# Two parts of the activations in one product of 512 columns: w_out, w_xq, w_xo and w_down of a decoder block

## The chip, the cores and the metric

The kernel runs on one core of a Trainium2 chip. The metric is the device time of one execution, in microseconds (us); of several runs the median is given. Engines go by the profile's names: PE is TensorE's products, PEld its loads of stationary operands, DVE is VectorE, ACT ScalarE, POOL GpSimd, SP SyncE, which issues most transfers.

## What is computed

One block over 256 rows of width 1024, in float32: a mixer (pool groups beside causal attention), cross-attention over a memory of 256 rows, and a gated feed-forward net with a convolution of three taps. Each part adds to the residual x:

```python
x = x + concatenate([pool, attn], axis=-1) @ w_out        # 1024 x 1024
h = rms_norm(x, norm_xattn_g)
x = x + cross_attention(h, m, w_xq, w_xkv, ..., w_xo)      # q = h @ w_xq; ... o @ w_xo, both 1024 x 1024
h = rms_norm(x, norm_ffn_g)
x = x + conv_ffn(h, w_up, conv_w, conv_b, w_down)          # up: 1024 x 5632; (silu(gate) * val) @ w_down: 2816 x 1024
```

## The kernel before

PE multiplies in float32r, which keeps fewer bits than float32. So each operand is split into a high part h (the value cast to float32r) and a low part l (what is left), and a product is three: h by h, h by l and l by h. ACT casts the high part and DVE subtracts for the low part, for activations (`part_h`, `part_l`, L237 to L247) and for weights alike (`split_h`, L185; `split_l`, L196). Weights come as `wpack`, chunks of two units; a unit is 128 x 1024, eight blocks of 128 x 128. `need(u)` (L198) issues transfers and splits ahead of unit u, by `look` units.

The stages of this text keep activations transposed: a feature block of 128 partitions by 256 rows (S). `b_tile` (L691) makes one output block f: for each of 8 input blocks k (22 in w_down) it calls `three`, whose products are L256 (weights' h by activations' h), L257 (weights' h by activations' l) and L258 (weights' l by activations' h). The weights are the stationary operand, the activations stream, 256 columns at a time, and all 24 (66) products go to one half of a bank of PSUM. Eight banks take turns. Pairs of activations live in two sets of four buffers, one for h and one for l (`pair`).

What empties a bank:

- w_out and w_xo, `resid_stage` (L702): DVE adds the bank to the residual (L709); ACT and DVE split the result times a gain into the next stage's operand (`evac_split`, ACT L241, DVE L247); ACT squares it (L712, L715); POOL sums the squares over the blocks (L716).
- w_xq (the loop before `value_job`): ACT and DVE split the bank straight into xq (L241, L247); ACT squares it (L801), POOL adds pairs of squares (L805).
- w_down (the last loop): DVE adds the bank and the residual into o (L936), and SP stores o (L937).

The order is by program: each engine does what it is given in that order. Work aside from the products (scores, softmax, splits of other tiles, the row sums over all blocks, L272) lies in generators, which are moved one step on by `tick()`, called after every second input block, and which wait so many ticks as the tables `WAIT_...` say. The row sums of w_out's squares are issued right behind the first output block of w_xq; those of w_xo's squares six ticks into w_up. The key job, which runs beside w_out, has DVE scale keys (L659), PE transpose them (L667) and ACT and DVE split them. An order of the stages: w_in, keys, w_out, w_xq, the value chunk (L357, L358, L361: products of 512 columns, where weights stream), w_xo, w_up, w_down.

Of the kernel before, what the change touches and what calls it, by code (L numbers as in the profile page):

```python
# [16 lines left out]
P = 128  # L17
# [8 lines left out]
XH = 4  # L26
# [48 lines left out]
def block_kernel(ctx: ExitStack, tc: tile.TileContext, wpack: bass.AP, scal: bass.AP, memT: bass.AP,  # L75
# [22 lines left out]
        return temps.tile([P, S], F32, name=name, tag="t1", bufs=8)  # L98

    def pair(name, cols=KT * S):  # L100
        h = pairs.tile([P, cols], F32R, name=name + "_h", tag="ph", bufs=4)
        l = pairs.tile([P, cols], F32R, name=name + "_l", tag="pl", bufs=4)
        return h, l

    def sm(name, n, dtype=F32):
        return small.tile([P, n], dtype, name=name)
# [147 lines left out]
    def three(o, stat, mov, start, stop):  # L254
# [2 lines left out]
        pe.matmul(o, stat[0], mov[1], start=False, stop=False)  # L257
        pe.matmul(o, stat[1], mov[0], start=False, stop=stop)  # L258

    def col(t, c):  # L260
        return t[:, c:c + 1]

    def tiles(p, k=KT):
        return [t.rearrange("p (k s) -> p k s", k=k) for t in p]

    rows = {}

# [66 lines left out]
    load_chunk(2, (0, 1024, 2048))  # L334
    nc.sync.dma_start(tab, table)
    nc.sync.dma_start(sc[:, C_GMEM:], scal[:, C_GMEM:])
    xgv = tiles(pair("xg"))

    def first_splits():
        for k in range(KT):  # L340
# [9 lines left out]
    def a_chunk(u0, actv, bk):  # L350

        for k in range(KT):
            w = need(u0 + k // 2)
            wv = [t[:, (k % 2) * 512:(k % 2) * 512 + 512] for t in w]
            a = [[t[:, k, tt * P:(tt + 1) * P] for t in actv] for tt in range(TT)]
            for tt in range(TT):
                pe.matmul(bk[tt], a[tt][0], wv[0], start=k == 0, stop=False)  # L357
                pe.matmul(bk[tt], a[tt][1], wv[0], start=False, stop=False)  # L358
            tick()
            for tt in range(TT):  # L360
                pe.matmul(bk[tt], a[tt][0], wv[1], start=False, stop=k == KT - 1)  # L361
            tick()
# [74 lines left out]
            pool.tensor_scalar(sneg, s, -(HD ** -0.5), None, op0=ALU.mult)  # L437
        yield from wait(WAIT_QK[5])

    qk = pairs.tile([P, KT * S], F32, name="qkT", tag="ph", bufs=4)  # L440
    j_of = {"q": 0, "k": 1}

    def stat_job():
# [33 lines left out]
            yield from wait(WAIT_MEM[0])  # L477
            part_l(mgv[1][:, k], r, mgv[0][:, k], col(sc, C_GMEM + k))

    mgv = tiles(pair("mg"))  # L480
    job_v = go(v_job())
    job_m = go(mem_job())
    stat_m = go(row_stat("m", mem_tile))
# [97 lines left out]
    bu = [bank(), bank()]  # L581
    look[0] = LOOKS[3]
    a_chunk(12, xgv, bu)
    cat = tiles(pair("cat"))


    def pool_job():
# [89 lines left out]
    look[0] = LOOKS[4]  # L677
    a_chunk(18, mgv, bk0)
    finish(job_k)
    kxv = tiles(pair("kx"))  # L680
    job_key0 = go(key_job(0, bk0))
    bk1 = [bank(), bank()]
    look[0] = LOOKS[5]
# [4 lines left out]

    halves = [0]

    def b_tile(u0, f, blocks, b, mov):  # L691

        for k in range(blocks):
            i = f * blocks + k
            w = need(u0 + i // 8)
            wv = [t[:, (i % 8) * P:(i % 8 + 1) * P] for t in w]
            three(b, wv, mov(k), k == 0, k == blocks - 1)
            halves[0] += 1
            if halves[0] % 2 == 0 and k < blocks - 1:
                tick()  # L700

    def resid_stage(u0, actv, gain, name, phase, held):  # L702
        hv = tiles(pair(name))
        acc = t1(name + "_acc")
        for f in range(KT):
            b = bank()[:, 0:S]
            look[0] = HOLD[2] if f >= KT - HOLD[held] else LOOKS[phase]
            b_tile(u0, f, KT, b, lambda k: [t[:, k] for t in actv])
            dve.tensor_tensor(resid[:, f], b, resid[:, f], op=ALU.add)  # L709
            evac_split(hv[0][:, f], hv[1][:, f], resid[:, f], col(sc, gain + f))  # L710
            if f == 0:
                act.activation(acc, resid[:, f], AF.Square)  # L712
            else:
                sq = t1(f"{name}_sq{f}")
                act.activation(sq, resid[:, f], AF.Square)  # L715
# [5 lines left out]
    h1, acc1 = resid_stage(26, cat, C_GX, "h1", 6, 0)  # L721


    xqv = tiles(pair("xq"))
    sqp = {}
    r1 = []
    ptv = []
# [7 lines left out]
    def x_job(hp):  # L735

        hs = (2 * hp, 2 * hp + 1)
        yield from after(job_key0, job_key, *job_r1)
        bs = [bank() for _ in range(TT)]
        for tt in range(TT):  # L740
            for i, h in enumerate(hs):
                o = bs[tt][:, i * XD:(i + 1) * XD]
                for dd in range(2):
                    q = [t[:, 2 * h + dd, tt * P:(tt + 1) * P] for t in xqv]
                    three(o, q, [t[:, 2 * h + dd] for t in kxv], dd == 0, dd == 1)
            if tt == 0:
                b = bank()
                for t in range(TT):
                    for i, h in enumerate(hs):
                        pe.matmul(b[:, 2 * t + i:2 * t + i + 1], sqp[h][:, t * P:(t + 1) * P], ones, start=True,  # L750
                                  stop=True)
            yield from wait(WAIT_X[0])
            if tt == 0:
                s2 = head_scale(f"hx{hp}", b, 2, XD, r1[0])
                pool.tensor_scalar(s2, s2, XD ** -0.5, None, op0=ALU.mult)
        pvs = []
        mx, nb, sums2, rec = (sm(f"{n}{hp}", 2 * TT) for n in ("xmx", "xnb", "xsum", "xrec"))
# [12 lines left out]
        yield from wait(WAIT_X[2])  # L770
        for tt in range(TT):
            c = slice(2 * tt, 2 * tt + 2)
            dve.reciprocal(rec[:, c], sums2[:, c])
            for j in range(2):
                dve.tensor_scalar(pvs[tt][:, j], pvs[tt][:, j], col(rec, 2 * tt + j), None, op0=ALU.mult)
            yield from wait(WAIT_X[3])
        yield from wait(WAIT_X[4])
        if not ptv:
            ptv.extend(t.rearrange("p (h m q) -> p h m q", h=XH, m=TT) for t in pair("xpt"))
        for j, h in enumerate(hs):  # L780
            b = bank()
            bb = b.rearrange("p (m q) -> p m q", m=TT)
            for mt in range(TT):
                for tt in range(TT):
                    pe.transpose(bb[:, mt, tt * P:(tt + 1) * P], pvs[tt][:, j, mt * P:(mt + 1) * P], ident)
            yield from wait(WAIT_X[5])
            part_h(ptv[0][:, h], bb)
            yield from wait(WAIT_X[6])
            part_l(ptv[1][:, h], bb, ptv[0][:, h])
        yield from wait(WAIT_X[7])  # L790

    jobs_x = []
    for f in range(KT):
        b = bank()[:, 0:S]
        b_tile(34, f, KT, b, lambda k: [t[:, k] for t in h1])
        if f == 0:
            job_r1.append(go(r1_job()))
        part_h(xqv[0][:, f], b, col(ggx, f % 2))
        part_l(xqv[1][:, f], b, xqv[0][:, f], col(ggx, f % 2))
        sq = t1(f"xsq{f}")  # L800
# [15 lines left out]

    def value_job(c, bks):
        for mt in range(TT):
            o = [t[:, mt, c * 512:(c + 1) * 512] for t in vxv]
            part_h(o[0], bks[mt], col(rows["m"], mt))  # L820
            part_l(o[1], bks[mt], o[0], col(rows["m"], mt))
        yield from wait(WAIT_VALUE[0])
# [1 line left out]
    bv0 = [bank(), bank()]  # L824
    look[0] = LOOKS[8]
    a_chunk(42, mgv, bv0)
    vxv = [t.rearrange("p (m d) -> p m d", m=TT) for t in pair("vx")]
    go(value_job(0, bv0))
    bv1 = [bank(), bank()]
    a_chunk(46, mgv, bv1)  # L830
    oxv = tiles(pair("ox"))
    finish(*jobs_x)
    go(value_job(1, bv1))
    for h in range(XH):
        b = bank()
        for dd in range(2):
            o = b[:, dd * S:(dd + 1) * S]
            for mt in range(TT):
                v = [t[:, mt, h * XD + dd * P:h * XD + (dd + 1) * P] for t in vxv]
                three(o, v, [t[:, h, mt] for t in ptv], mt == 0, mt == TT - 1)  # L840
        evac_split(oxv[0][:, 2 * h:2 * h + 2], oxv[1][:, 2 * h:2 * h + 2], b.rearrange("p (d s) -> p d s", d=2))

    h2, acc2 = resid_stage(50, oxv, C_GFFN, "h2", 9, 1)
# [31 lines left out]
    def up_job(i, b, scaled):  # L875
# [25 lines left out]
        h, l = (t[:, i % 8] for t in acts[i // 8])  # L901
        part_h(h, sg[:, S:])
        yield from wait(WAIT_UP[5])
        part_l(l, sg[:, S:], h)
# [4 lines left out]
    for i in range(NFF):  # L909
        b = bank()  # L910
        if i == 0:
            hs2 = tiles(pair("hs2"))
            job_r2.append(go(r2_job()))
        scaled = i >= SCALED
        hv = hs2 if scaled else h2
        if i == SCALED:
            finish(job_r2[0])
        for g in range(2):
            b_tile(58, 2 * i + g, KT, b[:, g * S:(g + 1) * S], lambda k: [t[:, k] for t in hv])
            if g == 0:  # L920
                tick()
        if i % 8 == 0:
            acts.append(tiles(pair(f"act{i // 8}")))
        jobs_up.append(go(up_job(i, b, scaled)))
        tick()

    def act_tile(k):
        finish(jobs_up[k])
        return [t[:, k % 8] for t in acts[k // 8]]

    look[0] = LOOKS[11]
    for f in range(KT):
        b = bank()[:, 0:S]
        b_tile(102, f, NFF, b, act_tile)
        o = t2(f"o{f}")[:, 0:S]
        dve.tensor_tensor(o, b, resid[:, f], op=ALU.add)  # L936
        nc.sync.dma_start(out[:, f], o)  # L937


# [90 lines left out]
```

## Time and profile before

| | |
|---|---|
| median of 3 runs | 396.2 us (396.15 to 396.35) |
| the profiled execution, its own time | 396.11 us |
| its span, first to last instruction | 394.3 us |
| busy PE, PEld, DVE, ACT, POOL | 98%, 93%, 72%, 59%, 24% of the span |
| granted TensorE clock | 1.00 of 2.4 GHz |
| share of PE in the chain that ended last | 76% |
| share of L256, L257 and L258 in it | 23% each |

The span is the time that the trace covers; 1.8 us of the execution lie around it. A shown duration of a product is longer than the step to the next one, since products are pipelined; the step is what counts. So it is with DVE and ACT, whose neighbours can overlap by their tails. In a row of the timeline "x2" stands for two instructions drawn as one, and the bracket at the end says how long the engine had been idle before it and whom it waited for.

### The profile page before, as it was taken

The page shows a single profiled execution, that of the slowest core. Times are in us where ns is not written, and L with a number is a line of the kernel's source. Part 1 is how long each engine was busy: PE and PEld are TensorE (multiplying, and loading weights), DVE is VectorE, ACT ScalarE, POOL GpSimd, SP SyncE. Part 2 cuts the span into 40 slices and gives each one's busy share as a digit, 9 for nine tenths or more (in the row PEclk, how much of TensorE's full clock was granted, in tenths as well). Part 3 has the DMA queues.
Part 4 walks back from the last instruction along what each step waited for, and adds up shares of the span by engine and source line. Part 5 has one row for each costly group of instructions (what it writes and reads, how often), then busy time and mean ns, then how long its engine had stood idle before and what let it go on. Part 6 is the DMA issues. An engine that isn't in the chain of part 4 may idle for free.

```text
span 394.3 us, 7288 instructions
## 1 busy us (share of the span) xinstructions
PE 387.3 (98%) x2892; PEld 367.9 (93%) x2892; DVE 283.8 (72%) x478; ACT 231.6 (59%) x421; POOL 93.9 (24%) x174
## 2 busy tenths in 40 slices
PE   7999999999999999999999999999999999999996
PEld 6888888888999998899999999999999999999996
DVE  4798989957767658857775999998877874553350
ACT  4775796966466546845654498765665676342210
POOL 0383884184252324000647300000000000000000
PEclk9999999999999999999999999999999999999999
DMA  8995381452325626253545236665554453364400
GB/s 266 423 344 200 114 315 60 168 199 96 121 107 214 214 106 227 101 208 106 170 155 213 108 108 219 229 250 181 189 213 164 166 206 108 131 229 169 180 17 23
DMA packets 12274, 69.22 MB, mean 176 GB/s; under 512 B 1360, under 2 KB 2768, under 8 KB 4688
## 3 DMA queue, kind: packets, MB, share of 16 engines
q1 hardware_dynamic: 11952, 68.24, 47.2%
q10 hardware_dynamic: 288, 0.52, 0.5%
q8 instruction: 22, 0.36, 0.4%
q14 instruction: 12, 0.10, 0.1%
HBM read 67.71 MB, written 1.05 MB: 174 GB/s over the span
## 4 chain that ended last, share of the span: by engine, by line
PE 76%; DVE 9%; DMA 5%; POOL 4%; ACT 3%; issue 3%; SPq 0%; DVEq 0%; ACTq 0%; POOLq 0%
PE bank L256 23%; PE bank L258 23%; PE bank L257 23%; DMA raw<-wpack 3%; DVE wl L196 3%; PE bank L357 2%; PE bank L361 2%; PE bank L358 2%; DMA sc<-scal 1%; ACT wh L185 1%; POOL rs4t L219 1%; DVE p L531 1%; DVE mg_l L247 1%; ACT p L527 1%; DVE mxs L520 0%
## 5 line engine op out<-in xcount | busy, mean ns | idle before, releaser
L196 DVE TENSOR_TENSOR wl<-raw,wh 128x1024 fp32r<-128x1024 f32 (+1 forms) x126 | 151.4, 1218 | 4.8 <-ACT wh L185 3.5
L185 ACT CAST wh<-raw 128x1024 fp32r<-128x1024 f32 (+1 forms) x125 | 123.8, 1024 | 38.3 <-DMA raw<-wpack 36.9
L256 PE MATMUL bank<-hs_h,wh 128*128 128x256 f32 x288 | 81.5, 283 | 0.0
L257 PE MATMUL bank<-hs_l,wh 128*128 128x256 f32 x288 | 81.5, 283 | 0.0
L258 PE MATMUL bank<-hs_h,wl 128*128 128x256 f32 x288 | 81.5, 283 | 0.0
L256 PEld LDWEIGHTS bank<-hs_h,wh 128*128 128x128 f32 x288 | 55.3, 192 | 0.0
L257 PEld LDWEIGHTS bank<-hs_l,wh 128*128 128x128 f32 x288 | 55.3, 192 | 0.0
L258 PEld LDWEIGHTS bank<-hs_h,wl 128*128 128x128 f32 x288 | 55.3, 192 | 0.0
L256 PE MATMUL bank<-act_h,wh 128*128 128x256 f32 x176 | 49.8, 283 | 0.0
L257 PE MATMUL bank<-act_l,wh 128*128 128x256 f32 x176 | 49.8, 283 | 0.0
L258 PE MATMUL bank<-act_h,wl 128*128 128x256 f32 x176 | 49.8, 283 | 0.0
L893 DVE SCALAR_TENSOR_TENSOR y<-bank,sc,y 128x255 f32<-128x255 f32 (+1 forms) x72 | 29.7, 474 | 14.4 <-ACT y L886 14.4
L256 PE MATMUL bank<-h_h,wh 128*128 128x256 f32 x128 | 36.6, 286 | 0.0
L258 PE MATMUL bank<-h_h,wl 128*128 128x256 f32 x128 | 36.2, 283 | 0.0
L257 PE MATMUL bank<-h_l,wh 128*128 128x256 f32 x128 | 36.2, 283 | 0.0
L886 ACT ACTIVATE y<-bank,sc 128x256 f32<-128x256 f32 x36 | 18.3, 559 | 27.6 <-PE bank L258 27.6
L256 PEld LDWEIGHTS bank<-act_h,wh 128*128 128x128 f32 x176 | 33.8, 192 | 0.0
L257 PEld LDWEIGHTS bank<-act_l,wh 128*128 128x128 f32 x176 | 33.8, 192 | 0.0
L258 PEld LDWEIGHTS bank<-act_h,wl 128*128 128x128 f32 x176 | 33.8, 192 | 0.0
L716 POOL TENSOR_TENSOR h_acc<-h_sq,h_acc 128x256 f32<-128x256 f32 x14 | 18.9, 1346 | 45.6 <-ACT h_sq L715 45.6
L936 DVE TENSOR_TENSOR o<-bank,sc 128x256 f32<-128x256 f32 x8 | 3.4, 425 | 35.3 <-PE bank L258 35.3
L357 PE MATMUL bank<-wh,xg_h 128*128 128x512 f32 x64 | 26.1, 408 | 1.8 <-DVE wh L185 1.8
(244 smaller groups left out, 864.4 us busy)
## 6 DMA issues: line engine op xcount, KB each, us to landing
raw<-wpack SPq DMA_DIRECT2D x59, 1024.0 KB, 4.8
raw<-wpack SPq DMA_DIRECT2D x4, 512.0 KB, 7.3
mraw<-memT SPq DMA_DIRECT2D x4, 256.0 KB, 7.4
out<-o SPq DMA_DIRECT2D x8, 128.0 KB, 1.9
raw<-wpack ACTq DMA_DIRECT2D x2, 256.0 KB, 4.5
raw<-wpack SPq DMA_DIRECT2D x2, 256.0 KB, 5.6
sc<-scal SPq DMA_DIRECT2D x1, 512.0 KB, 6.8
tab<-table SPq DMA_DIRECT2D x1, 480.0 KB, 9.1
```

The lines of the kernel that those rows point to most:

```text
L185: copy(split[u][0][:, r], unit(u)[:, r])
L196: dve.tensor_tensor(l[:, r], unit(u)[:, r], h[:, r].bitcast(F32), op=ALU.subtract)
L219: pool.tensor_tensor(t, y, y, op=ALU.mult)
L256: pe.matmul(o, stat[0], mov[0], start=start, stop=False)
L257: pe.matmul(o, stat[0], mov[1], start=False, stop=False)
L258: pe.matmul(o, stat[1], mov[0], start=False, stop=stop)
L357: pe.matmul(bk[tt], a[tt][0], wv[0], start=k == 0, stop=False)
L358: pe.matmul(bk[tt], a[tt][1], wv[0], start=False, stop=False)
L361: pe.matmul(bk[tt], a[tt][0], wv[1], start=False, stop=k == KT - 1)
L716: pool.tensor_tensor(acc, sq, acc, op=ALU.add)
L886: act.activation(y[:, g * S:(g + 1) * S], src[:, g * S:(g + 1) * S], AF.Identity, bias=col(sc, C_CB + f), scale=col(sc, C_CW + 2 * 2 * NFF ...
L893: dve.scalar_tensor_tensor(yy[:, j:], uu[:, :S - j], col(sc, C_CW + (2 - j) * 2 * NFF + f), yy[:, j:], op0=ALU.mult, op1=ALU.add)
```

## The change

In the four stages the two parts of the activations stream as one product: for each block of weights there is one product of 512 columns (weights' h by both parts, into the two halves of a bank) and one of 256 (weights' l by the activations' h, into the first half), in place of three of 256. The first block goes 512 then 256, the others 256 then 512. Both parts now lie in one buffer, h first and l behind it, so that a view with two pieces takes both; four buffers of double size replace the two sets of four. w_up and the other products keep `three`.

On emptying, the halves are added. In `resid_stage` and in w_down DVE adds twice, first one half to the residual and then the other half to the result. In w_xq ACT copies the second half to a new buffer of 256 columns, DVE adds the first half to it, and the split and the square read that buffer in place of the bank.

```diff
     def pair(name, cols=KT * S):
-        h = pairs.tile([P, cols], F32R, name=name + "_h", tag="ph", bufs=4)
-        l = pairs.tile([P, cols], F32R, name=name + "_l", tag="pl", bufs=4)
-        return h, l
+        return pairs.tile([P, 2 * cols], F32R, name=name, tag="pair", bufs=4)
...
+    def both(b, stat, mov, start, stop):
+        if start:
+            pe.matmul(b, stat[0], mov, start=True, stop=False)
+            pe.matmul(b[:, 0], stat[1], mov[:, 0], start=False, stop=False)
+        else:
+            pe.matmul(b[:, 0], stat[1], mov[:, 0], start=False, stop=False)
+            pe.matmul(b, stat[0], mov, start=False, stop=stop)
...
-    def b_tile(u0, f, blocks, b, mov):
+    def b_tile(u0, f, blocks, b, mov, product=both):
...
-            three(b, wv, mov(k), k == 0, k == blocks - 1)
+            product(b, wv, mov(k), k == 0, k == blocks - 1)
...
+    def two_parts():
+        return bank().rearrange("p (z s) -> p z s", z=2)
...
-            b = bank()[:, 0:S]
+            b = two_parts()
             look[0] = HOLD[2] if f >= KT - HOLD[held] else LOOKS[phase]
-            b_tile(u0, f, KT, b, lambda k: [t[:, k] for t in actv])
-            dve.tensor_tensor(resid[:, f], b, resid[:, f], op=ALU.add)
+            b_tile(u0, f, KT, b, lambda k: actv[2][:, :, k])
+            for z in range(2):
+                dve.tensor_tensor(resid[:, f], b[:, z], resid[:, f], op=ALU.add)
...
-        b = bank()[:, 0:S]
-        b_tile(34, f, KT, b, lambda k: [t[:, k] for t in h1])
+        bb = two_parts()
+        b_tile(34, f, KT, bb, lambda k: h1[2][:, :, k])
         if f == 0:
             job_r1.append(go(r1_job()))
+        b = t1(f"xq{f}")
+        act.copy(b, bb[:, 1])
+        dve.tensor_tensor(b, bb[:, 0], b, op=ALU.add)
...
-        b = bank()[:, 0:S]
+        b = two_parts()
         b_tile(102, f, NFF, b, act_tile)
         o = t2(f"o{f}")[:, 0:S]
-        dve.tensor_tensor(o, b, resid[:, f], op=ALU.add)
+        for z, add in enumerate((resid[:, f], o)):
+            dve.tensor_tensor(o, b[:, z], add, op=ALU.add)
```

The rest of the diff passes the new views (h, l, both) to what used the old pairs.

## Rows read from the trace of the kernel before

**Rows 1.** PE's waits over the span: who waited for whom, total us, times, longest.

```profile
PE bank L256 <- DVE cat_l L247: 0.5, 1, 0.5
```

**Rows 2.** Timeline, PE, w_down's first and last product: start us, us, instruction.

```profile
327.42 0.28 PE L256 MATMUL bank<-act_h,wh 128*128 128x256 f32 x1
...
390.65 0.28 PE L258 MATMUL bank<-act_h,wl 128*128 128x256 f32 x1
```

**Rows 3.** The chain in order of time, value chunk: start us, us, what.

```profile
145.13 0.23 PE bank L357
...
149.22 0.44 PE bank L785 x4
```

**Rows 4.** Lines L613 (one piece) and L614 (two): ns min/median/max, first and last start.

```profile
L613 PE MATMUL bank<-misc,ul x4: 280/281/285, 61.3 to 71.4; 128*128 128x256 f32 x4
...
L614 PE MATMUL bank<-maskr,uh x4: 277/280/284, 61.4 to 71.5; 128*128 128x256 f32 x4
```

**Rows 5.** Timeline, DVE: xnb reads xmx; the split behind o's add is independent.

```profile
142.94 0.68 DVE L761 TENSOR_REDUCE xmx<-bank 128x2 f32<-128x512 f32 x1
143.74 0.16 DVE L762 SCALAR_TENSOR_TENSOR xnb<-xmx,rs7y 128x2 f32<-128x2 f32 x1
143.82 0.69 DVE L761 TENSOR_REDUCE xmx<-bank 128x2 f32<-128x512 f32 x1
144.54 0.16 DVE L762 SCALAR_TENSOR_TENSOR xnb<-xmx,rs7y 128x2 f32<-128x2 f32 x1
...
335.54 0.42 DVE L936 TENSOR_TENSOR o<-bank,sc 128x256 f32<-128x256 f32 x1 [3.20 <-PE bank L258]
335.88 3.49 DVE L196 TENSOR_TENSOR wl<-raw,wh 128x1024 fp32r<-128x1024 f32 x3
```

**Rows 6.** Timeline, DVE, w_out: keys scaled, adds of tiles 1, 6 and 7.

```profile
99.16 0.87 DVE L659 TENSOR_SCALAR kn<-bank,rs6y 128x256 f32<-128x256 f32 x2 [1.78 <-POOL rs6y L222]
...
101.08 0.42 DVE L709 TENSOR_TENSOR sc<-bank,sc 128x256 f32<-128x256 f32 x1
...
113.41 0.42 DVE L709 TENSOR_TENSOR sc<-bank,sc 128x256 f32<-128x256 f32 x1
...
115.84 0.42 DVE L709 TENSOR_TENSOR sc<-bank,sc 128x256 f32<-128x256 f32 x1 [0.95 <-PE bank L258]
```

**Rows 7.** Timeline, from w_out to w_xq: sums of squares and row sums.

```profile
114.82 0.74 POOL L716 TENSOR_TENSOR h_acc<-h_sq,h_acc 128x256 f32<-128x256 f32 x1 [0.66 <-ACT h_sq L715]
...
117.24 2.90 DVE L196 TENSOR_TENSOR wl<-raw,wh 128x1024 fp32r<-128x1024 f32 x2
117.25 1.81 POOL L716 TENSOR_TENSOR h_acc<-h_sq,h_acc 128x256 f32<-128x256 f32 x1 [1.69 <-ACT h_sq L715]
...
119.11 0.19 PEld L272 LDWEIGHTS bank<-ones,h_acc 128*128 128x128 f32 x1 [0.21 <-POOL h_acc L716]
```

**Rows 8.** Timeline, ACT, w_xq: a square, and the next tile's high part.

```profile
126.70 0.38 ACT L801 ACTIVATE xsq<-bank 128x256 f32<-128x256 f32 x1 [0.61 <-DVE xq_l L247]
...
128.50 0.47 ACT L241 ACTIVATE xq_h<-bank,ggx 128x256 fp32r<-128x256 f32 x1 [0.47 <-PE bank L258]
```

**Rows 9.** Timeline, w_xo: PE's first product, adds 0, 1, 2 and 7, w_up's start.

```profile
176.78 0.28 PE L256 MATMUL bank<-ox_h,wh 128*128 128x256 f32 x1
...
179.86 0.42 DVE L709 TENSOR_TENSOR sc<-bank,sc 128x256 f32<-128x256 f32 x1 [0.44 <-PE bank L258]
...
182.74 0.42 DVE L709 TENSOR_TENSOR sc<-bank,sc 128x256 f32<-128x256 f32 x1 [0.26 <-PE bank L258]
...
185.85 0.41 DVE L709 TENSOR_TENSOR sc<-bank,sc 128x256 f32<-128x256 f32 x1
...
199.82 0.28 PE L256 MATMUL bank<-h_h,wh 128*128 128x256 f32 x1
...
200.02 0.42 DVE L709 TENSOR_TENSOR sc<-bank,sc 128x256 f32<-128x256 f32 x1 [1.39 <-PE bank L258]
201.03 0.48 DVE L247 SCALAR_TENSOR_TENSOR h_l<-sc,h_h 128x256 fp32r<-128x256 f32 x1 [0.58 <-ACT h_h L241]
```

More of the change, by code (lines that the diff above doesn't have):

```diff
@@ L258, in three, with tiles @@
         pe.matmul(o, stat[1], mov[0], start=False, stop=stop)
+    def both(b, stat, mov, start, stop):
[5 more added lines that the diff above has]
+            pe.matmul(b, stat[0], mov, start=False, stop=stop)
     def col(t, c):
         return t[:, c:c + 1]
-    def tiles(p, k=KT):
-        return [t.rearrange("p (k s) -> p k s", k=k) for t in p]
+    def tiles(t, *dims):
+        names = " ".join("abc"[:len(dims) - 1]) + " s"
+        sizes = dict(zip("abc", dims[:-1]))
+        v = t.rearrange(f"p (z {names}) -> p z {names}", z=2, **sizes)
+        return v[:, 0], v[:, 1], v
     rows = {}
@@ L336, in block_kernel @@
     nc.sync.dma_start(sc[:, C_GMEM:], scal[:, C_GMEM:])
-    xgv = tiles(pair("xg"))
+    xgv = tiles(pair("xg"), KT, S)
     def first_splits():
@@ L354, in a_chunk @@
             wv = [t[:, (k % 2) * 512:(k % 2) * 512 + 512] for t in w]
-            a = [[t[:, k, tt * P:(tt + 1) * P] for t in actv] for tt in range(TT)]
+            a = [[t[:, k, tt * P:(tt + 1) * P] for t in actv[:2]] for tt in range(TT)]
             for tt in range(TT):
@@ L438, in qk_job @@
         yield from wait(WAIT_QK[5])
-    qk = pairs.tile([P, KT * S], F32, name="qkT", tag="ph", bufs=4)
+    qk = pairs.tile([P, KT * S], F32, name="qkT", tag="pair", bufs=4)
     j_of = {"q": 0, "k": 1}
@@ L478, in mem_job @@
             part_l(mgv[1][:, k], r, mgv[0][:, k], col(sc, C_GMEM + k))
-    mgv = tiles(pair("mg"))
+    mgv = tiles(pair("mg"), KT, S)
     job_v = go(v_job())
@@ L583, in block_kernel @@
     a_chunk(12, xgv, bu)
-    cat = tiles(pair("cat"))
+    cat = tiles(pair("cat"), KT, S)
     def pool_job():
@@ L679, in block_kernel @@
     finish(job_k)
-    kxv = tiles(pair("kx"))
+    kxv = tiles(pair("kx"), KT, S)
     job_key0 = go(key_job(0, bk0))
@@ L700, in b_tile @@
                 tick()
+    def two_parts():
+        return bank().rearrange("p (z s) -> p z s", z=2)
     def resid_stage(u0, actv, gain, name, phase, held):
[L703 removed]
+        hv = tiles(pair(name), KT, S)
         acc = t1(name + "_acc")
         for f in range(KT):
[L706 removed]
+            b = two_parts()
             look[0] = HOLD[2] if f >= KT - HOLD[held] else LOOKS[phase]
[L708 to L709 removed]
+            b_tile(u0, f, KT, b, lambda k: actv[2][:, :, k])
+            for z in range(2):
+                dve.tensor_tensor(resid[:, f], b[:, z], resid[:, f], op=ALU.add)
             evac_split(hv[0][:, f], hv[1][:, f], resid[:, f], col(sc, gain + f))
@@ L721, in block_kernel @@
     h1, acc1 = resid_stage(26, cat, C_GX, "h1", 6, 0)
-    xqv = tiles(pair("xq"))
+    xqv = tiles(pair("xq"), KT, S)
     sqp = {}
@@ L743, in x_job @@
                 for dd in range(2):
-                    q = [t[:, 2 * h + dd, tt * P:(tt + 1) * P] for t in xqv]
-                    three(o, q, [t[:, 2 * h + dd] for t in kxv], dd == 0, dd == 1)
+                    q = [t[:, 2 * h + dd, tt * P:(tt + 1) * P] for t in xqv[:2]]
+                    three(o, q, [t[:, 2 * h + dd] for t in kxv[:2]], dd == 0, dd == 1)
             if tt == 0:
@@ L778, in x_job @@
         if not ptv:
-            ptv.extend(t.rearrange("p (h m q) -> p h m q", h=XH, m=TT) for t in pair("xpt"))
+            ptv.extend(tiles(pair("xpt"), XH, TT, S))
         for j, h in enumerate(hs):
@@ L818, in value_job @@
         for mt in range(TT):
-            o = [t[:, mt, c * 512:(c + 1) * 512] for t in vxv]
+            o = [t[:, mt, c * 512:(c + 1) * 512] for t in vxv[:2]]
             part_h(o[0], bks[mt], col(rows["m"], mt))
@@ L826, in block_kernel @@
     a_chunk(42, mgv, bv0)
-    vxv = [t.rearrange("p (m d) -> p m d", m=TT) for t in pair("vx")]
+    vxv = tiles(pair("vx"), TT, XH * XD)
     go(value_job(0, bv0))
@@ L830, in block_kernel @@
     a_chunk(46, mgv, bv1)
-    oxv = tiles(pair("ox"))
+    oxv = tiles(pair("ox"), KT, S)
     finish(*jobs_x)
@@ L838, in block_kernel @@
             for mt in range(TT):
-                v = [t[:, mt, h * XD + dd * P:h * XD + (dd + 1) * P] for t in vxv]
-                three(o, v, [t[:, h, mt] for t in ptv], mt == 0, mt == TT - 1)
+                v = [t[:, mt, h * XD + dd * P:h * XD + (dd + 1) * P] for t in vxv[:2]]
+                three(o, v, [t[:, h, mt] for t in ptv[:2]], mt == 0, mt == TT - 1)
         evac_split(oxv[0][:, 2 * h:2 * h + 2], oxv[1][:, 2 * h:2 * h + 2], b.rearrange("p (d s) -> p d s", d=2))
@@ L900, in up_job @@
         yield from wait(WAIT_UP[4])
-        h, l = (t[:, i % 8] for t in acts[i // 8])
+        h, l = (t[:, i % 8] for t in acts[i // 8][:2])
         part_h(h, sg[:, S:])
@@ L911, in block_kernel @@
         if i == 0:
-            hs2 = tiles(pair("hs2"))
+            hs2 = tiles(pair("hs2"), KT, S)
             job_r2.append(go(r2_job()))
@@ L918, in block_kernel @@
         for g in range(2):
-            b_tile(58, 2 * i + g, KT, b[:, g * S:(g + 1) * S], lambda k: [t[:, k] for t in hv])
+            b_tile(58, 2 * i + g, KT, b[:, g * S:(g + 1) * S], lambda k: [t[:, k] for t in hv[:2]], three)
             if g == 0:
@@ L922, in block_kernel @@
         if i % 8 == 0:
-            acts.append(tiles(pair(f"act{i // 8}")))
+            acts.append(tiles(pair(f"act{i // 8}"), KT, S))
         jobs_up.append(go(up_job(i, b, scaled)))
@@ L928, in act_tile @@
         finish(jobs_up[k])
-        return [t[:, k % 8] for t in acts[k // 8]]
+        return acts[k // 8][2][:, :, k % 8]
     look[0] = LOOKS[11]
     for f in range(KT):
-        b = bank()[:, 0:S]
+        b = two_parts()
         b_tile(102, f, NFF, b, act_tile)
         o = t2(f"o{f}")[:, 0:S]
-        dve.tensor_tensor(o, b, resid[:, f], op=ALU.add)
+        for z, add in enumerate((resid[:, f], o)):
+            dve.tensor_tensor(o, b[:, z], add, op=ALU.add)
         nc.sync.dma_start(out[:, f], o)
```

## The prediction

> **What bounds the kernel now.** I read the page's busy shares first, then its chain of waits, then who waited for whom on PE, then stretches of the timeline. The shares and the chain put PE far ahead. The view of PE's waits says it more sharply: from the start of w_out to the last product PE's products wait 0.5 us, for cat_l at that start [rows 1]. So in w_out, w_xq, w_xo and w_down a product less is time less, as long as what empties the banks keeps up. One execution gives all durations: it took 396.11 us around a span of 394.3, which is 0.09 under the median of the runs (396.2). I work out a difference and put it on the median.
>
> **What a product costs.** In w_down the first product starts at 327.42 and the last, the 528th, at 390.65 [rows 2]: 63.23 us over 527 steps, 120.0 ns for 256 columns with a weight load of its own. The 512-column products of the value chunk, each with its own load too, stand 18 steps apart between 145.13 and 149.22 [rows 3]: 227.2 ns. A block of weights costs 3 x 120.0 = 360.0 ns now and 227.2 + 120.0 = 347.2 after: 12.8 ns less. There are 64 blocks in each of w_out, w_xq and w_xo and 176 in w_down, 368 in all: 4.71 us less (0.82 each, 2.25 in w_down). That the moving operand comes in two pieces (high and low part, 8 KB apart) I cost at nothing: a product whose moving operand is two pieces of maskr takes a median of 280 ns where its neighbour with one piece takes 281 [rows 4]. Loads of wl stand behind 512 columns and loads of wh behind 256, as all do now.
>
> The trace makes the fixed part of a product 13 to 14 ns: 120.0 less 256 columns at 2.4 GHz (106.7), and 227.2 less 213.3. The Trainium skill (TensorE: Matmul & The Clock Gate, Wait — 56ns, not 53.3ns?) puts the fixed cost of a product in a stream at 2.5 ns at full clock, which speaks against this change: by it a product less is worth 368 x 2.5 ns = 0.92 us, not 4.71. The rows differ from it at both sizes, so the sum goes by the rows.
>
> **What a second add costs.** The first product leaves h's sum and l's sum in two halves of a bank, so DVE adds twice: bank to resid (or o), then the other half to the result. The second reads what the first wrote. Call X the time from the first add's start to the second's. An operation that needs nothing of the one before follows the o add after 0.34 us, though that add shows 0.42 [rows 5]: the tails overlap. An operation that reads its predecessor's result does not overlap: the xnb product starts 0.03 us after the end of the maximum that it reads in one place and 0.12 after it in the other [rows 5]. So X is 0.34 at least, 0.42 + 0.03 = 0.45 likeliest, 0.54 at most; I take 0.45, since the second add waits for the first by construction. Queued behind the waiting add are, on DVE, the low part h_l (L247) and the weight split (L196), and through them ACT's h_h (L241) and square, POOL's sum of squares (L716), and PE where it reads them.
>
> **w_out.** DVE, not PE, is short of room here. It works in order; after an idle 1.78 us at 99.16 (which takes in what the first tile's second add costs) the adds of tiles 1 to 6, of which the first starts at 101.08 and the last at 113.41, run behind PE: between them DVE is busy or waits for ACT's h_h, and only before the add of tile 7 (they count from 0) does it wait for PE again, 0.95 us [rows 6]. Six second adds push the last first add back by 6X, its own second add pushes what follows by one more: 7X = 3.15 us against a slack of 0.95, so 2.20 us late. What follows is the square, POOL's last addition and then the row sums (L272), for which PE already waits 0.21 us [rows 7]. PE's own saving of 0.82 does not help, since the chain on DVE doesn't start earlier: the row sums come 7X - 0.95 = **+2.20 us** later than now. The wait for h_l of tile 7, at the eighth block of the next stage, lies within this one. POOL's last addition takes 1.81 us beside the weight split that started 0.01 us before it, and 0.74 where none runs [rows 7]; I keep 1.81.
>
> **w_xq.** A copy on ACT and an add on DVE come before the split of each tile. ACT's round had 0.47 us to spare of 2.88, and its square waited 0.61 for DVE to leave the bank, which ends as it now reads SBUF [rows 8]. With a copy (0.38, the square's length), and the wait for the add (0.46) the round is 2.41 + 0.38 + 0.46 - 0.61 = 2.64 of the new 2.78: it just fits, and scores on xq follow eight ticks (16 blocks, 5.6 us) after tile 3. Were it over, splits of weights would come late, two tiles after. Seven tiles behind the row sums save 7 x 8 x 12.8 ns = **-0.72 us**.
>
> **w_xo.** The same chain, with more room. PE starts at 176.78 and the first add at 179.86 [rows 9]; 24 products shorter by 0.10 put it at 179.76. From one add to the next DVE needs 182.74 - 0.26 - 179.86 = 2.62 us, once 185.85 - 182.74 = 3.11 (a split beside POOL's addition), and before the last, where no weights are split, 2.88 - 1.39 = 1.49 [rows 9]. The last add starts at 179.76 + 2.62 + 3.11 + 4 x 2.62 + 1.49 + 7X = 200.61, where PE would allow 199.20. Its h_l ends 1.49 us after the add begins (200.02 to 201.51) [rows 9], plus X: 202.55. PE starts w_up at 199.82 - 0.82 = 199.00 and wants that low part 21 products and one later, at 201.64. So PE waits 8X - 2.69 = 0.91 us: -0.82 + 0.91 = **+0.09 us**.
>
> **w_down.** DVE idles 3.2 us before an o add [rows 5]; nothing waits: **-2.25 us**. Behind the last product nothing hides the second add: **+0.45 us**. Longer tenure of a bank costs nothing: eight rotate. Merging h and l into one buffer moves no wait, as both parts were written and given up together, and the same four live at once; xq's new buffers are given up within their tile. No DMA is added or moved.
>
> Sum: +2.20 - 0.72 + 0.09 - 2.25 + 0.45 = -0.23 us. On the median: **396.0 us**, no change. About 0.2% (0.8 us) is what can be told from none. For this case alone, X between 0.42 and 0.50, the sum runs from -0.7 to +0.6.
>
> **Rivals.** *The second add overlaps the first* (X = 0.34), as any neighbour does. Then w_out costs 1.43, w_xo gains 0.79, the tail 0.34: 1.43 - 0.72 - 0.79 - 2.25 + 0.34 = -1.99, **394.2 us**. For it: the o add's row; against: both dependent pairs [rows 5]. The Trainium skill (VectorE: DVE Perf Modes, The DRAIN you can't avoid) says that a semaphore between chained operations costs nothing extra; by that rule dependent and independent neighbours would stand equally far apart, which is this case. The rows show them apart by 0.1 us. Chance 0.17.
>
> *POOL's last addition starts before the split* and takes 0.74: row sums 1.07 us sooner, -1.30, **394.9 us**. For it: the gap of 0.01 us [rows 7]; against: the change moves both alike. Chance 0.12.
>
> *The chain on DVE isn't binding at all* and the whole saving arrives: -4.71 + 0.45, **391.9 us**. Against it stands the wait of 0.21 us at the row sums, there before anything is added [rows 7]. Chance 0.05.
>
> *Slower: the second add waits its dear price.* Its place is the chain of w_out and w_xo, its price X = 0.54, as with the later of the two pairs [rows 5]. Then 2.83 - 0.72 + 0.81 - 2.25 + 0.54 = +1.21, **397.4 us**. Each 0.01 of X is worth 0.16 us (seven adds in w_out, eight in w_xo, one at the end), so it decides from X = 0.515, where the sum passes +0.8. For it: two adds of 256 columns with a read from PSUM were never chained in this trace. Chance 0.18.
>
> *The 512-column product doesn't do what it says*: two pieces stream like two products, 240 ns. Nothing is saved, the adds stay: 2.20 for w_out, 0.2 for w_xo, 0.45 at the end, +2.85, **399.0 us**. Against: the rows of both sizes and of the two pieces [rows 2 to 4]. Chance 0.04. (By the skill's 2.5 ns above it would be 398.4.)
>
> **How the numbers follow.** The forecast has 0.44. Faster by over 0.2%: 0.17 + 0.12 + 0.05, and a little of the forecast's lower edge: 0.36. Slower: 0.18 + 0.04: 0.22. Within: 0.42. The range leaves out the whole saving below and the useless product above with a part of the slower rival: 394.0 to 397.5; the forecast's own is 395.5 to 396.8.
>
> **What would show it.** Steps of 0.227 and 0.120 us in the four stages. The second L709 0.45 us after the first. In w_out no wait of DVE for PE at the last tile; PE waiting some 3 us for h_l and h_acc between the start of w_xq and the row sums, then at 121.3 us; PE waiting 0.9 us for h_l early in w_up; w_down 61.0 us long. The forecast is wrong if PE runs through both boundaries, if X is 0.34, or if PE waits for weights or banks.

## The result and the profile after

The changed kernel takes 398.22 us (median of 14 runs, 396.21 to 401.34), the kernel before 396.17 beside it (14 runs, 395.15 to 396.89): ratio 1.0062, 95% interval 1.0047 to 1.0077. It is slower by 2 us, and where the runs of before lie within 1.7 us, its own spread over 5. Its profiled execution took 397.14 us, with a span of 395.4.

| from | to | before, us | after | change | forecast |
|---|---|---|---|---|---|
| span's start | w_out's first product | 91.20 | 91.40 | +0.20 | 0 |
| there | row sums behind w_out | 27.91 | 29.98 | +2.07 | +2.20 |
| there | w_xo's first product | 57.67 | 57.13 | -0.54 | -0.72 |
| there | w_down's first product | 150.64 | 150.70 | +0.06 | +0.09 |
| there | first add of the last o | 63.55 | 62.33 | -1.22 | -2.25 |
| there | the end | 3.36 | 3.82 | +0.46 | +0.45 |
| sum | | 394.33 | 395.36 | +1.03 | -0.23 |

Five of the six stages came out close to forecast; w_down gave 1 us less than it should. The +0.20 ahead of w_out is no part of the change: over all profiles of this text w_out starts anywhere from 90.82 to 92.11 us. And the table is one execution, 1.0 us over before where the medians are 2 us apart: the rest is not in this profile.

VectorE in w_out, timeline (start us, us, instruction):

```profile
115.81 0.88 DVE L725 TENSOR_TENSOR sc<-bank,sc 128x256 f32<-128x256 f32 x2
...
117.67 0.88 DVE L725 TENSOR_TENSOR sc<-bank,sc 128x256 f32<-128x256 f32 x2
```

Both adds of tiles 6 and 7. The wait of 0.95 us for PE before tile 7's add [rows 6] is gone: DVE's chain, not PE, now sets the pace.

TensorE and POOL at the boundary to w_xq, timeline; in brackets the idle time before and its releaser:

```profile
119.14 0.38 PE L265 MATMUL bank<-h,wl 128*128 128x256 f32 x1 [0.84 <-ACT h L240]
...
121.38 0.61 PE L284 MATMUL bank<-ones,h_acc 128*128 128x1 f32 x4 [1.22 <-POOL h_acc L732]
```

```profile
119.54 1.78 POOL L732 TENSOR_TENSOR h_acc<-h_sq,h_acc 128x256 f32<-128x256 f32 x1 [1.12 <-ACT h_sq L731]
```

The row sums start at 121.38, for 119.11 before [rows 7]. PE stands twice in close succession, 0.84 us for tile 7's high part and 1.22 us for POOL's last addition. In PE's waits over the span (total us, times, longest) both are new beside [rows 1]:

```profile
PE bank L284 <- POOL h_acc L732: 1.2, 1, 1.2
...
PE bank L265 <- ACT h L240: 0.8, 1, 0.8
PE bank L262 <- DVE cat L246: 0.5, 1, 0.5
```

The row of w_xo and w_up hides two parts. From w_xo's first product to w_up's first the time falls from 23.04 to 22.37 us (-0.67, forecast -0.82); from there to w_down's first it grows from 127.59 to 128.33 (+0.74, forecast a wait of 0.91 for h_l). The largest part of the second is one step in w_up, 0.52 us where products stand 0.12 apart:

```profile
203.39 0.38 PE L255 MATMUL bank<-h,wh 128*128 128x256 f32 x1
203.91 0.39 PE L256 MATMUL bank<-h,wh 128*128 128x256 f32 x1
```

w_down, timeline of PE, first product and steps in the middle, then the tail on DVE and SP's queue:

```profile
329.21 0.40 PE L262 MATMUL bank<-act,wh 128*128 128x512 f32 x1
...
345.56 0.40 PE L266 MATMUL bank<-act,wh 128*128 128x512 f32 x1
345.80 0.28 PE L265 MATMUL bank<-act,wl 128*128 128x256 f32 x1
345.92 0.40 PE L266 MATMUL bank<-act,wh 128*128 128x512 f32 x1
346.15 0.28 PE L265 MATMUL bank<-act,wl 128*128 128x256 f32 x1
```

```profile
391.54 0.42 DVE L956 TENSOR_TENSOR o<-bank,sc 128x256 f32<-128x256 f32 x1 [5.75 <-PE bank L266]
392.00 0.43 DVE L956 TENSOR_TENSOR o<-bank,o 128x256 f32<-128x256 f32 x1
392.45 0.33 SPq L957 DMA_DIRECT2D out<-o  x1
```

The second add starts 0.46 us after the first: X = 0.46. The step behind a product of 512 columns is 0.23 to 0.24 us, behind one of 256 it is 0.12. The stage is 1.22 us shorter over 176 blocks: 6.9 ns a block, not 12.8.

### The profile page after: what moved, and what is told of

The parts are those of the page before. It is cut to its first block, busy times and chain, and to the rows that moved or that the text cites. A ratio compares the mean times of both kernels' runs of the same rounds, so it can differ in the third digit from the quotient of the medians.

```text
span 395.4 us, 6590 instructions
## 1 busy us (share of the span) xinstructions
PE 385.9 (98%) x2524; PEld 348.7 (88%) x2524; DVE 297.5 (75%) x510; ACT 233.3 (59%) x429; POOL 91.3 (23%) x174
## 4 chain that ended last, share of the span: by engine, by line
PE 80%; DVE 11%; POOL 4%; ACT 2%; issue 1%; DMA 1%; POOLq 0%
PE bank L266 13%; PE bank L256 12%; PE bank L257 11%; PE bank L255 11%; PE bank L369 7%; PE bank L265 7%; PE bank L370 7%; PE bank L373 7%; DVE wl L195 4%; DVE sc L725 3%; ACT h L240 2%; DVE h L246 2%; PE bank L262 1%; DMA sc<-scal 1%; DVE kn L671 1%
## 5 line engine op out<-in xcount | busy, mean ns | idle before, releaser
L255 PE MATMUL bank<-hs,wh 128*128 128x256 f32 x288 | 81.5, 283 | 0.0
L256 PE MATMUL bank<-hs,wh 128*128 128x256 f32 x288 | 81.5, 283 | 0.0
L257 PE MATMUL bank<-hs,wl 128*128 128x256 f32 x288 | 81.5, 283 | 0.0
L266 PE MATMUL bank<-act,wh 128*128 128x512 f32 x168 | 59.7, 399 | 0.0
L255 PEld LDWEIGHTS bank<-hs,wh 128*128 128x128 f32 x288 | 55.3, 192 | 0.0
L256 PEld LDWEIGHTS bank<-hs,wh 128*128 128x128 f32 x288 | 55.3, 192 | 0.0
L257 PEld LDWEIGHTS bank<-hs,wl 128*128 128x128 f32 x288 | 55.3, 192 | 0.0
L265 PE MATMUL bank<-act,wl 128*128 128x256 f32 x168 | 47.2, 281 | 0.0
L266 PEld LDWEIGHTS bank<-act,wh 128*128 128x128 f32 x168 | 31.6, 188 | 7.5
L265 PEld LDWEIGHTS bank<-act,wl 128*128 128x128 f32 x168 | 31.8, 189 | 0.3
L369 PE MATMUL bank<-wh,xg 128*128 128x512 f32 x64 | 26.4, 413 | 1.5 <-DVE wh L184 1.5
L369 PE MATMUL bank<-wh,mg 128*128 128x512 f32 x64 | 26.1, 408 | 0.0
L370 PE MATMUL bank<-wh,xg 128*128 128x512 f32 x64 | 25.9, 405 | 0.0
L370 PE MATMUL bank<-wh,mg 128*128 128x512 f32 x64 | 25.0, 391 | 0.0
```

The source lines that it names most:

```text
L255: pe.matmul(o, stat[0], mov[0], start=start, stop=False)
L265: pe.matmul(b[:, 0], stat[1], mov[:, 0], start=False, stop=False)
L266: pe.matmul(b, stat[0], mov, start=False, stop=stop)
```

## Experiments

The theory after reading the profile had two parts. *The clock*: the pair of waits at the row sums lets TensorE's granted clock fall in some executions, and that is the part of the loss that the profile lacks. *The block*: a block of weights, now a pair of products, saves 6 to 8 ns. Rivals: the second add costs more than the profile shows; the pieces of the moving operand disturb PE; the 512-column products themselves lower the clock. Each group of runs has its own runs of the kernel before; those beside the first four had a median of 395.82 us (17 runs).

**The changed kernel once more,** unaltered.

> The changed kernel, unaltered, to see its spread and its granted clock. Theory A (PE's wait at the start of w_xq, some 2 us from 118.2 to 121.4, lets the clock fall in many executions): median near 398.2 within 396.2 to 401.4; executions with a mean clock of 1.00 at 396.2 to 397.2, those with 0.99 at 399 to 401; in a profile with a clock under 1.00 the stretch of lower clock begins within a few us of 121. Rival B (the clock falls where the products of 512 columns stand, because weight loads are fewer): the lower stretch lies in w_out, w_xo or w_down, and not behind that wait.

Measured: 399.13 us (396.17 to 399.96, 6 runs), ratio 1.0072 (1.0045 to 1.0099). This time the profile caught a long execution, 399.96 us. Its stretches, beside the same stretches of the first profile of the changed kernel (window, its length, busy PE, PEld, DVE, ACT, POOL, granted clock, DMA share, GB/s). First the profile above:

```profile
120.00:121.50 1.50, 0.28 (x2) 0.13 (x2) 1.50 (x2) 1.50 (x3) 1.32 (x1) 1.00 0.00 0
121.50:124.00 2.50, 2.50 (x16) 2.27 (x17) 1.92 (x5) 1.09 (x4) 0.22 (x1) 1.00 0.84 269
124.00:126.00 2.00, 2.00 (x13) 1.73 (x12) 2.00 (x3) 1.46 (x3) 0.00 (x0) 1.00 0.45 188
126.00:128.00 2.00, 2.00 (x14) 1.74 (x13) 1.42 (x4) 1.43 (x3) 0.53 (x1) 1.00 0.38 66
```

And the long execution of the same code:

```profile
120.00:121.50 1.50, 0.28 (x3) 0.28 (x2) 1.50 (x2) 1.50 (x3) 1.17 (x1) 0.93 0.00 0
121.50:124.00 2.50, 2.50 (x10) 2.31 (x10) 1.92 (x5) 1.09 (x4) 0.22 (x1) 0.50 0.92 285
124.00:126.00 2.00, 2.00 (x7) 1.68 (x7) 2.00 (x3) 1.04 (x2) 0.00 (x0) 0.50 0.40 168
126.00:128.00 2.00, 2.00 (x8) 1.65 (x7) 0.05 (x1) 0.37 (x1) 0.00 (x0) 0.50 0.40 57
128.00:132.00 4.00, 4.00 (x24) 3.53 (x24) 2.96 (x4) 2.53 (x6) 0.74 (x1) 0.99 0.55 233
```

Up to the row sums the two agree (waits of 0.83 and 1.22 us, row sums at 121.23). Then the granted clock is 0.50, the lower of its two levels (1.2 GHz), from the end of the wait to 128 us, with PE called busy throughout: 8 products are drawn between 126 and 128 us where 14 were. From the row sums to w_xo's first product (181.43) this execution takes 60.20 us instead of 57.13: 3.07 us for the clock alone. Of the six runs one had a mean granted clock of 1.00, and it took 396.17 us; the others had 0.990 to 0.993 and took 397.79 to 399.96. Of the 14 runs above, five had 0.998 or more and took 396.21 to 397.44; nine had less and took 397.61 to 401.34.

**The second add left out** in w_out and w_xo (the low parts' half of the bank is never added there).

```diff
-            for z in range(2):
-                dve.tensor_tensor(resid[:, f], b[:, z], resid[:, f], op=ALU.add)
+            dve.tensor_tensor(resid[:, f], b[:, 0], resid[:, f], op=ALU.add)
```

> The second add of w_out and w_xo is left out (the product of the weights' high part with the activations' low part does not reach the residual). Theory A: DVE's chain is as short as before, PE's wait at the row sums falls from 2 us to 0.2, the clock stays 1.00, and the blocks' saving of 6 to 8 ns in 368 blocks arrives less 0.5 at the tail: 396.2 - 2.4 + 0.5 = 394.3, with a spread of under 1 us. Rival B: the same wait gone, but the clock still falls in many executions: 394 to 398, median 396.

Measured: 393.66 us (393.03 to 394.05, 6 runs), ratio 0.9945 (0.9932 to 0.9958), granted clock 0.998 to 1.00 in every run. Neither wait at the row sums is left, and these come at 118.20 for a start of w_out at 90.87: 27.33 us, 0.58 under before. So with PE setting the pace w_out gains 0.58 us, and the sixteen adds are what turned a gain of 2.2 us into a loss.

**One piece instead of two:** high and low part of each block side by side, so that 512 columns stream as one run.

```diff
-        v = t.rearrange(f"p (z {names}) -> p z {names}", z=2, **sizes)
+        v = t.rearrange(f"p ({names[:-1]}z s) -> p z {names}", z=2, **sizes)
```

> High and low part of a block lie side by side, so the product of 512 columns reads one piece instead of two that are 8 KB apart. If the two pieces are what costs 0.235 us in place of 0.227: the step falls to 0.227, w_down to 61.1 us, and the time by 1.0 there and 0.3 in w_xq: 1.3 us under the changed kernel, 396.9. Rival (a product of 512 behind one of 256 waits for its weights): the step stays at 0.235 and the time at 398.2.

Measured: 399.26 us (396.87 to 400.84, 6 runs), ratio 1.0075 (1.0047 to 1.0102): as the changed kernel. Timeline of PE in w_down:

```profile
345.40 0.40 PE L266 MATMUL bank<-act,wh 128*128 128x512 f32 x1
345.63 0.28 PE L265 MATMUL bank<-act,wl 128*128 128x256 f32 x1
345.75 0.40 PE L266 MATMUL bank<-act,wh 128*128 128x512 f32 x1
```

The pair takes 0.35 us as before. Two pieces cost nothing; that rival is out.

**The wait filled:** five products of 512 columns, which nobody reads, ahead of the row sums. They give PE work in the wait and end no chain sooner.

```diff
         yield from wait(WAIT_R1[0])
+        d = two_parts()
+        for _ in range(5):
+            pe.matmul(d, split[34][0][:, 0:P], h1[2][:, :, 0], start=True, stop=True)
```

> Five extra products of 512 columns into a spare bank stand before the row sums, where PE waits for POOL anyway (1.2 us); nothing reads them. Theory A: the row sums come no later, PE idles less there and the clock stays 1.00 in more executions: 396.5 to 397.5. Rival B: the spread stays, median 398.2. If the wait were not POOL's but PE's own lateness, the time would grow by 1.2 us.

Measured: 396.63 us (395.97 to 397.95, 12 runs), ratio 1.0023 (1.0013 to 1.0034), granted clock 0.998 to 1.00 in all twelve. Stretches, and timeline of PE:

```profile
120.00:121.50 1.50, 1.36 (x6) 0.99 (x7) 1.50 (x3) 1.50 (x3) 1.27 (x1) 1.00 0.00 0
121.50:124.00 2.50, 2.43 (x15) 1.84 (x14) 2.50 (x4) 1.23 (x3) 0.66 (x2) 1.00 0.53 151
```

```profile
119.83 0.38 PE L265 MATMUL bank<-h,wl 128*128 128x256 f32 x1 [0.83 <-ACT h L240]
...
122.09 0.61 PE L284 MATMUL bank<-ones,h_acc 128*128 128x1 f32 x4
```

The row sums stand 29.98 us behind w_out's start (92.11), to the hundredth where they stood; the wait for h is still 0.83. Only PE's idleness before them is gone, and with it the low clock and 2.5 us. This settles the clock's part: products that do nothing make the kernel faster. What is left, 0.8 us over before, is the stage table's sum from w_out on, +0.83.

The next four shared runs of the kernel before with a median of 396.11 us (23 runs).

**The change in w_xq and w_down alone.** In w_out and w_xo:

```diff
-            b_tile(u0, f, KT, b, lambda k: actv[2][:, :, k])
-            for z in range(2):
-                dve.tensor_tensor(resid[:, f], b[:, z], resid[:, f], op=ALU.add)
+            b_tile(u0, f, KT, b, lambda k: [t[:, k] for t in actv[:2]], three)
+            dve.tensor_tensor(resid[:, f], b, resid[:, f], op=ALU.add)
```

> The change in w_xq and w_down alone; w_out and w_xo keep three products and one add, so VectorE's chain is that of the kernel before and TensorE waits no longer than before ahead of the row sums. Theory (the loss is VectorE's chain in w_out and the clock that falls after it; the product saves 6 to 8 ns a block where TensorE sets the pace): w_xq -0.4, w_down -1.2, tail +0.5, so about -1.1 us against the kernel before (ratio 0.997), granted clock 1.00 and a narrow spread. Rival (the 512-column products themselves disturb the clock or the time): still slower than before, 398 to 399.

Measured: 394.57 us (394.08 to 396.00, 12 runs), ratio 0.9962 (0.9951 to 0.9974), clock 0.996 to 1.00. Faster than before, as expected. Row sums to w_xo's first product: 119.45 to 176.52, 57.07 us, 0.60 under before.

**The change in w_down alone:** as above, and `three` with the old emptying in w_xq.

> The change in w_down alone. Theory: -1.2 in w_down and +0.5 at the tail, so about -0.7 us (ratio 0.998); the difference to the kernel with w_xq and w_down is then w_xq's share, about 0.4 us. By the prediction's 12.8 ns a block: -2.25 + 0.45, so -1.8 us (ratio 0.9955). Rival (the 512-column product gains nothing in w_down): +0.5 us.

Measured: 395.15 us (394.66 to 395.84, 12 runs), ratio 0.9978 (0.9968 to 0.9988). It hits the expected 0.998 and not the 0.9955 of the prediction's 12.8 ns.

**Products grouped by kind** in w_xq and w_down: four of 512 columns, four of 256, then the kinds in the other order, so that runs of eight arise.

```diff
+            for wide in ((True, False) if n % 2 == 0 else (False, True)):
+                for k, wv, m in zip(ks, ws, ms):
+                    if wide:
+                        pe.matmul(b, wv[0], m, start=k == 0, stop=k == blocks - 1)
+                    else:
+                        pe.matmul(b[:, 0], wv[1], m[:, 0], start=False, stop=False)
```

> As the change in w_xq and w_down alone, with the products of four blocks grouped by kind there: four of 512 columns, four of 256, the order of kinds turned about from group to group. In the changed kernel a pair takes 0.2345 to 0.2365 us and 0.116 to 0.118 us, where rows of before gave 227.2 and 120.0 ns. Theory (the extra of the 512-column product belongs to a step from a narrow product to a wide one, which here comes in a quarter of the blocks or less): w_down's 176 blocks about 347 ns each, so w_down some 1 us under that of the ungrouped kernel, ratio about 0.994. Rival (every 512-column product costs 0.235 beside these weight loads, whatever stands before it): w_down the same within 0.2 us, ratio as the ungrouped kernel.

Measured: 394.28 us (393.52 to 394.87, 6 runs), ratio 0.9952 (0.9936 to 0.9968). Timeline of PE in w_down; x8 are eight products drawn as one:

```profile
335.67 1.11 PE L727 MATMUL bank<-act,wl 128*128 128x256 f32 x8
336.62 2.00 PE L725 MATMUL bank<-act,wh 128*128 128x512 f32 x8
338.46 1.12 PE L727 MATMUL bank<-act,wl 128*128 128x256 f32 x8
339.41 2.00 PE L725 MATMUL bank<-act,wh 128*128 128x512 f32 x8
```

Eight wide products take 1.84 us, 230 ns each, and eight narrow 0.95, 119 ns each: 349 ns a pair. From the first product to the first add of the last o w_down takes 61.69 us (327.06 to 388.75), 1.86 under before, or 10.6 ns a block, and 0.64 under the changed kernel. I had expected some 1 us, so the theory holds by two thirds: most of what was missing in w_down goes away when the widths don't alternate there. The medians of the grouped and ungrouped kernel (0.9952 and 0.9962) overlap in their intervals; the stage's length tells them apart.

But alternating is not dear everywhere. In w_xo of the changed kernel (the first profile), where the same two products alternate, the first products of output blocks 1, 2 and 3 stand so:

```profile
181.33 0.40 PE L262 MATMUL bank<-ox,wh 128*128 128x512 f32 x1
...
184.10 0.39 PE L262 MATMUL bank<-ox,wh 128*128 128x512 f32 x1
...
186.92 0.40 PE L262 MATMUL bank<-ox,wh 128*128 128x512 f32 x1
```

Output block 1 takes 2.77 us and output block 2 takes 2.82: 346 and 352 ns for each of the eight blocks of weights, and so by turns through the stage. In w_down every output block takes 7.77 us for its 22, 353 ns each. So the alternating stream has two rhythms. The faster is the 347.2 ns that I had summed, and it is faster than the grouped products' 349; w_down stays in the slower one. Both are there in every profile of the changed kernel. What picks the rhythm no run shows.

**The add without the products:** the kernel before, with one more dependent instruction on VectorE behind each add to resid.

```diff
             dve.tensor_tensor(resid[:, f], b, resid[:, f], op=ALU.add)
+            dve.tensor_tensor(resid[:, f], resid[:, f], resid[:, f], op=ALU.max)
```

> The kernel before, products untouched, with one more dependent VectorE instruction behind each addition to resid (the maximum of resid with itself, which leaves the value). Theory (VectorE's chain in w_out ends late and TensorE's wait brings the clock down, and no product of 512 columns is needed for it): row sums about 2.2 us later, a wait of about 0.9 us at the start of w_up, and in many executions a granted clock of 0.5 for some microseconds behind the row sums: 398.5 to 401 us where the clock falls. Rival (the lone addition is harmless and the loss needs the 512-column products): 396 to 397, ratio under 1.002.

Measured: 401.06 us (400.15 to 402.88, 5 runs), ratio 1.0133 (1.0109 to 1.0156), granted clock 0.991 to 0.996 in all five. Waits of PE, then stretches:

```profile
PE bank L272 <- POOL h_acc L717: 1.2, 1, 1.2
...
PE bank L256 <- ACT h_h L241: 1.0, 1, 1.0
```

```profile
121.50:124.00 2.50, 2.45 (x11) 2.45 (x12) 2.50 (x5) 1.07 (x3) 0.22 (x1) 0.50 0.79 236
124.00:126.00 2.00, 2.00 (x12) 2.00 (x11) 1.36 (x2) 1.05 (x2) 0.00 (x0) 0.50 0.58 238
```

Two such waits and the same low clock, with the four stages' products left as they were: row sums at 121.55, 30.73 us behind w_out's start (90.82) and so 2.82 later than before, and 60.34 us from there to w_xo's first product (181.89), 2.67 over before. The rival that blames the wide products is out. The row sums come later than the expected 2.2 because the added instruction, which reads SBUF alone, takes a median of 0.51 us and up to 0.58. Of the expected wait of 0.9 us at w_up, 0.76 show in the stage's length: from w_up's first product to w_down's it is 128.35 us, for 127.59 before.

The last two shared runs of the kernel before with a median of 395.82 us (17 runs).

**The row sums four ticks later** in the changed kernel.

```diff
-        yield from wait(WAIT_R1[0])
+        yield from wait(4)
```

> The changed kernel with the row sums of w_xq issued four ticks later, so that TensorE has w_xq's products to do while POOL ends the sum; the wait for h (0.8 us) stays. Theory (the two waits of 0.8 and 1.2 us in close succession let the clock fall): the wait for POOL is gone, the clock stays at 1.00, 396 to 397 us, ratio 1.000 to 1.003, narrow like the kernel with extra products. Rival (the wait for h alone, or the change's products, lower the clock): 398 to 399, ratio 1.006.

Measured: 396.28 us (395.59 to 398.68, 12 runs), ratio 1.0013 (1.0000 to 1.0027). The wait for POOL is gone, and the median is the expected one. "The clock stays at 1.00" failed: nine runs had 0.998 or more and took 395.59 to 396.54, three had 0.989 to 0.996 and took 397.33 to 398.68. The profile caught one of the three, timeline of PE and then stretches:

```profile
118.62 0.39 PE L265 MATMUL bank<-h,wl 128*128 128x256 f32 x1 [0.81 <-ACT h L240]
...
120.28 0.38 PE L263 MATMUL bank<-h,wl 128*128 128x256 f32 x1 [0.40 <-DVE wl L195]
...
123.37 0.85 PE L284 MATMUL bank<-ones,h_acc 128*128 128x1 f32 x4
```

```profile
120.00:121.50 1.50, 1.22 (x6) 1.08 (x7) 1.50 (x2) 1.50 (x3) 0.81 (x1) 0.80 0.28 44
121.50:124.00 2.50, 2.50 (x11) 2.21 (x9) 1.93 (x5) 1.15 (x4) 0.00 (x0) 0.50 0.82 324
124.00:126.00 2.00, 2.00 (x12) 1.80 (x12) 2.00 (x4) 0.98 (x2) 0.22 (x1) 0.92 0.21 86
```

Another wait had moved up, 0.40 us for a low part of weights. So a mean clock under 0.998 stands in 3 executions of 12 with the waits of 0.81 and 0.40 us, in 14 of 20 with those of 0.84 and 1.22 (both sets of the changed kernel), and in none of 12 with that of 0.83 and the filled gap. A profile shows the place of the fall for one execution of each of the first two kinds; for the others it is inferred from mean clock and time. A count can be off by one or two: the change in w_xq and w_down alone had two executions at 0.996 that took no longer than the rest.

**Put together:** as the grouped kernel; the first four tiles of w_xo take wide products and two adds as well, and the last tile of w_down takes `three` and one add.

```diff
+            if phase == 9 and f < 4:
+                b = two_parts()
+                grouped(u0, f, KT, b, lambda k: actv[2][:, :, k])
...
+        else:
+            b = bank()[:, 0:S]
+            b_tile(102, f, NFF, b, lambda k: [acts[k // 8][z][:, k % 8] for z in range(2)], three)
+            dve.tensor_tensor(o, b, resid[:, f], op=ALU.add)
```

> As the kernel with w_xq and w_down grouped by kind, with two more edits: the first four tiles of w_xo take the grouped 512-column products and two adds too, and the last tile of w_down takes three products and one add. Theory: 32 blocks of w_xo at some 11 ns make 0.35 us, while four more adds (4 x 0.46 = 1.84) stay under the 2.69 us by which VectorE was ahead there; the tail wins 0.46 for one add and loses 22 x 11 ns = 0.24. So 0.5 to 0.6 us under the grouped kernel, ratio about 0.994. Rival (VectorE's extra work in w_xo comes out at w_up's start all the same): as the grouped kernel, 0.995 to 0.996.

Measured: 393.87 us (393.24 to 393.97, 5 runs), ratio 0.9943 (0.9931 to 0.9955), clock 0.999 to 1.00. The fastest of all that compute the whole, 2 us under before; its interval overlaps that of the grouped kernel, so the medians don't show what the last two edits add. The two profiles do: w_xo and w_up together take 150.28 us for 150.63 in the grouped kernel, and w_down with its tail 65.26 for 65.51, 0.60 us in all, as expected.

## Why the prediction was wrong

I forecast 396.0 us and no change; 398.22 lies outside the range of 394.0 to 397.5. Two steps failed.

**The sum has no term for the clock.** I forecast that PE would be "waiting some 3 us for h_l and h_acc between the start of w_xq and the row sums", and priced that wait by its length only. PE did wait, 2.06 us in two parts (for the high part and for h_acc), but behind it the granted clock is at 1.2 GHz in most executions, which costs 3.07 us in the one profiled: more than the wait itself. Before had its clock at 1.00 and no such pair of waits [rows 1], so no row of it gave the price; but the place was in my own sum, and I named neither a bound nor a rival for it. The filled wait, and the add without the products, show it from both sides. The Trainium skill (TensorE: Matmul & The Clock Gate, A second HAM failure mode: psum-queue depth-cycling) says of another kernel that frequent short idle spells of PE between groups of products make its clock go down and up again, at a cost in throughput. The runs agree in kind: here the clock fell and rose again behind two spells, of 0.83 and 1.22 us in the execution profiled.

**The block's saving of 12.8 ns was mis-sized.** It came from products of 512 columns among themselves [rows 3] and of 256 among themselves [rows 2]; the change alternates them. Alternating, w_down saves 6.9 ns a block, -1.22 us where I had -2.25; grouped by kind 10.6 ns, -1.86. So most of the error in w_down is a slower rhythm of the alternating stream, 353 ns a block, which neither row contained. The summed 347.2 does occur, in every second output block of w_xo; why w_down never falls into that rhythm stays open, and so do the 2.2 ns that are missing when grouped. The piece that I had costed at nothing, the operand in two pieces, did cost nothing. The Trainium skill (TensorE: Matmul & The Clock Gate, Wait — 56ns, not 53.3ns?) has a fixed cost of 2.5 ns for a product in a stream, so that by it one product less saves an estimated 2.5 ns a block. The 6.9 ns of w_down lie between that and my figure, and w_xo's faster output blocks reach mine.

The rest stood, in part by luck. X was 0.46 for 0.45. DVE's chain sets w_out's end: +2.07 for +2.20, and the row sums came at 121.38 for 121.3. POOL's last addition took 1.78 us, so the rival with 0.74 fell. The tail came to +0.46 for +0.45. w_xo with w_up came to +0.06 for +0.09, but there a smaller saving (-0.67 for -0.82) met a smaller loss (+0.74 for +0.91), and that the two misses cancel is luck. w_xq came to -0.54 for -0.72, which is 9.6 ns for each of its 56 blocks; like w_xo it saves more a block than w_down. With 6.9 ns in w_down and the rest as forecast the sum would have been +2.20 - 0.72 + 0.09 - 1.22 + 0.45 = +0.80; the profile at full clock shows +0.83 from w_out on, and the medians 2 us.

Of the rivals, "the dear price" (X = 0.54) had the right sign and place but not the mechanism. The useless product came near with its 399.0 by accident: the wide products do save time, as the kernels without the added chain show (0.9962 and 0.9978). "The chain on DVE isn't binding" fell with the row sums 2.07 us late; even the kernel with the second add left out in w_out and w_xo takes 393.66, not 391.9.

## What to carry to other kernels

A saving on the bounding engine that is paid for with work on a second one is worth taking only in stages where that second engine has slack; here the same edit wins in w_xq and w_down and loses in w_out. Where a change adds waits of TensorE between stages, as the 0.84 and 1.22 us here, price them twice, by their length and by a fall of the granted clock behind them, and look at several executions, since one profile can miss it. Take the step of a product from a row with the same neighbours: widths that alternate need not stand as far apart as the same widths among themselves, and here they had two rhythms.

## What was not expected

The same code kept its clock in 6 of 20 executions and lost it in the others, though in the two profiled, one of each kind, the waits agree to 0.01 us; what decides between them was not found. One added VectorE instruction on 16 tiles, a median of 0.51 us each and 7.8 us of busy time in all, on an engine idle for over a quarter of the span, cost 4.95 us (401.06 against 396.11). And five products without a reader saved 1.6 to 2.5 us of the changed kernel's time.
